# Seven products of a block in an order in which neighbours never share banks, and the convolution history turned in mid-block

## The chip, the cores and the metric

The kernel runs on one core of one Trainium2 chip. The metric is the time of one execution on the device in microseconds (us). The core has TensorE (matrix products, in the profile PE, and PEld for its weight loads), VectorE (DVE), ScalarE (ACT), GpSimd (POOL) and SyncE (SP), whose queue issues the transfers. Each engine works off its own list of instructions in order and waits for others through semaphores.

## What is computed

The reference is one inference step of a one-layer trunk with 1,024 prompt tokens and 8 x 4 sample tokens (`h` below is the normalised input, 1,056 tokens by 1,024 features). One projection of `h` feeds two branches; the second, a matrix memory with four heads, is the one that the change bears on:

```
pool_in, pool_z, qk_pre, v, o_pre, m_z, if_pre, gate_pre = jnp.split(h @ w_in, SPLIT_OFFSETS, axis=-1)
qk, conv_hist_new = causal_conv_silu(qk_pre, conv_hist, conv_w, conv_b)
q, k = jnp.split(qk, 2, axis=-1)

def causal_conv_silu(z, hist, w, b):
    S = z.shape[1]
    full = jnp.concatenate([hist.astype(z.dtype), z], axis=1)
    out = sum(full[:, j:j + S] * w[j] for j in range(CONV_W)) + b
    return jax.nn.silu(out), full[:, -(CONV_W - 1):]
```

`qk_pre` has 4,096 columns, `v`, `o_pre` and `m_z` 2,048 each, 512 for each head. The convolution has four taps, so that each sample sequence needs three rows of history (`state_conv`, 24 rows for 8 sequences), and the last three rows of each sequence are an output.

## The kernel before

The kernel runs in stages. The first, to about 950 us of the span, computes the ten thousand columns of `q`, `k`, `v`, `o_pre` and `m_z`; the stages behind it (gates, attention, the pooling branch, the output projections) are not touched.

**Blocks.** For each of the four heads there are seven blocks: `q` twice, `v`, `k` twice, `o`, `z` (line 1532 on). The blocks of `q` and `k` (ConvBlock, "feature blocks", 16 of them) put 256 output features on partitions and tokens on columns; those of `v`, `o` and `z` (TokBlock, "token blocks", 12) put tokens on partitions and 512 features on columns. A block is cut in two halves of tokens and two of features, and the four quarters are computed by Strassen and Winograd's scheme with seven products in place of eight. Every operand is kept as two parts, hi (`whi`, `hh`, `m2h`, ...) and lo (`wlo`, `hl`, `m2l`, ...), and a product is hi by hi, hi by lo and lo by hi: 24 matmuls of 264 columns in a feature block, and 48 matmuls of 256 columns in a token block.

**Products and banks.** The products are, by the letters of the new code, a (operand B11), 00 (B21), d (M1), b (M2), c (T3), 10 (N4) and 01 (B22). Each adds up in a pair of PSUM banks from `mm2()` (line 343; there are three pairs, `mm` in the trace). The "chain" pair takes a, then b, c and 10 on top of it; the pair `d` takes d and then 01; the pair `x` takes 00 alone. Before, the order is a, 00, d, b, c, 10, 01 (`run`, lines 76 to 103), so that b, c and 10, all of the chain, stand one behind the other. Behind a, b and c ScalarE copies the chain to SBUF (`save`, tile `s`: lines 158 to 161 in feature blocks, one instruction, and 215 to 219 in token blocks, two), and VectorE or ScalarE turns banks and saved sums into the four quarters (`bring`, tile `z`): quarter (0,0) from 00 and saved a, (1,1) from d's banks and saved c, (1,0) from the chain alone, (0,1) from d's banks after 01 and saved b.

**Weights.** `steps` (line 665) prepares the weights of a product three products ahead of it. `prep` adds and subtracts raw weight halves on VectorE; `split_w` makes `whi` on ScalarE (line 351) and `wlo` on VectorE (line 357), each in three rotating buffers. A feature block splits the weights of two products in one go: 00 with 10, d with b, 01 with c. The raw weights (`wraw`, seven buffers) come by DMA from SP's queue (line 653).

**Convolution.** When the weights of a feature block are asked for (`load`), `history` (line 269) also loads its 24 rows of history (tile `part`), turns them with two transposes on TensorE (line 277) and copies them to `hist`. `give` (line 285) puts the first three columns, the history and the samples in place on GpSimd and ScalarE, collects the rows of the new history in `new` on GpSimd (lines 297 and 300), and runs the taps on VectorE (line 305). At the end of the block `done` (line 312) turns `new` with two transposes (line 316) and stores it. Stores and loads share SP's queue.

**What sets the order.** The order in which the code is written is that of the products; a scheduler then places the instructions of each engine by simulated times, so that matmuls of the next block can stand between two products of this one.

Of the kernel before, what the change touches and what calls it, by code (L numbers as in the profile page):

```python
# [53 lines left out]
class Block:  # L54
# [7 lines left out]

    def __init__(self, tr, c0):
        self.tr, self.c0 = tr, c0
        self.w = [None] * 7
        self.saved = {}
        self.raw = [[], []]
        self.begin()
# [44 lines left out]
OPS = ("B11", "B21", "M1", "M2", "T3", "N4", "B22")  # L113


class FeatBlock(Block):


    def load(self, f):
        if f == 0:  # L120
            self.r = self.tr.raw_w(self.tr.I["w_in"], self.c0, 0)
            self.history()

    def history(self):
        pass

    def prep(self, i):
# [3 lines left out]
        if i == 0:  # L131
            self.w[0] = tr.split_w(r1[:, :, f1])
        elif i == 1:
            hi, lo = tr.split_w(r2)
            self.w[1], self.w[5] = [(hi[:, :, f], lo[:, :, f]) for f in (f1, f2)]
        elif i == 2:
# [4 lines left out]
            self.w[2], self.w[3] = [(hi[:, :, f], lo[:, :, f]) for f in (f1, f2)]  # L141
            tt(out=r1[:, :, f2], in0=r1[:, :, f1], in1=r1[:, :, f2], op=ALU.subtract)
            tt(out=r1[:, :, f1], in0=r2[:, :, f1], in1=x[:, :, f2], op=ALU.add)
        elif i == 4:
            hi, lo = tr.split_w(r1)
            self.w[6], self.w[4] = [(hi[:, :, f], lo[:, :, f]) for f in (f1, f2)]
# [11 lines left out]
    def save(self, name):  # L158
        tr = self.tr
        self.saved[name] = tr.t(tr.gp, [P, HH], "s", bufs=tr.nsb).rearrange("p (a n) -> p a n", a=2)  # L160
        tr.nc.scalar.activation(self.saved[name], self.chain[:, :, :CH], AF.Copy)
# [13 lines left out]
class TokBlock(Block):  # L175
# [15 lines left out]
    def prep(self, i):  # L191
        tr, r = self.tr, self.raw
        tt = tr.nc.vector.tensor_tensor
        if i == 2:
            self.x = tr.t(tr.wp, [P, 4, 256], "wraw", bufs=tr.nraw)
            tt(out=self.x, in0=r[0][1], in1=r[1][1], op=ALU.add)
        elif i == 3:
            tt(out=self.x, in0=r[0][0], in1=self.x, op=ALU.subtract)
        elif i == 4:
            tt(out=r[0][1], in0=r[0][0], in1=r[0][1], op=ALU.subtract)  # L200
        elif i == 6:
# [1435 lines left out]
```

## Time and profile before

| what | value |
|---|---|
| time, median of 3 runs | 2282.23 us (2280.12 to 2287.49) |
| the profiled execution, its time | 2283.02 us |
| its span in the profile | 2281.3 us |
| mean granted clock of TensorE | 0.987 of full speed |
| busy share TensorE, its weight loads | 95%, 90% |
| busy share VectorE, ScalarE, GpSimd | 55%, 41%, 6% |

The busy share is an average over all stages. A start time in a row of the timeline is in us from the start of the span; a name like `mm<-whi,t3h` says that the tile `mm` is written from the tiles `whi` and `t3h`; what stands in brackets is the idle time of the engine before the instruction and what ended it.

### The profile page before, as it was taken

The numbers are of one execution on the slowest core, as the hardware profiler recorded it, in microseconds if no ns is written. First come the engines' busy times: TensorE is split into PE (matmuls) and PEld (weight loads), VectorE is DVE, ScalarE is ACT, GpSimd is POOL, SyncE is SP. The second block draws the span as 40 slices with busy tenths as digits, with TensorE's granted clock in tenths as the row PEclk, the third lists the DMA queues.
The fourth block names the chain that finished last, engine by engine and source line by source line (L and its number), as shares of the span: only waits on it lengthen the run. The fifth ranks groups of instructions, "written<-read, shape, count | busy, mean of one in ns | idle before, by whom it ended". The sixth has DMA issues, their size and how long they took to land.

```text
span 2281.3 us, 39968 instructions
## 1 busy us (share of the span) xinstructions
PE 2162.9 (95%) x16311; PEld 2047.6 (90%) x16311; DVE 1259.2 (55%) x2168; ACT 927.3 (41%) x1796; POOL 136.1 (6%) x335
## 2 busy tenths in 40 slices
PE   4899999999999999999999999999998999999998
PEld 3899999999999999899999888878778999999998
DVE  7756465547554756435565765665582334443545
ACT  5536353635453546454333443322233331223443
POOL 1101010001000110000000000000000000000000
PEclk8999999999999999999999999999999999999999
DMA  3233323332323232384555563878674534324112
GB/s 127 80 109 102 112 77 108 101 107 82 108 92 98 93 97 74 95 271 153 185 179 163 172 192 121 300 247 287 249 241 173 171 96 130 104 70 138 52 47 82
DMA packets 238600, 312.70 MB, mean 137 GB/s; under 512 B 13994, under 2 KB 170066, under 8 KB 238416
## 3 DMA queue, kind: packets, MB, share of 16 engines
q1 hardware_dynamic: 238416, 310.15, 41.7%
q8 instruction: 128, 2.10, 0.4%
q14 instruction: 56, 0.46, 0.1%
HBM read 200.01 MB, written 110.45 MB: 136 GB/s over the span
## 4 chain that ended last, share of the span: by engine, by line
PE 83%; DMA 7%; ACT 3%; DVE 3%; SPq 1%; issue 1%; POOL 0%; DVEq 0%; POOLq 0%; ACTq 0%
PE mm L211 20%; PE mm L154 14%; PE mm L364 12%; PE mm L366 11%; PE mm L365 11%; PE num L1121 2%; PE misc L906 1%; PE num L364 1%; PE num L365 1%; PE num L366 1%; DMA o<-oD 1%; PE kv L364 1%; DMA ct<-state_mlstm_C 1%; PE kv L1125 1%; PE kv L365 1%
## 5 line engine op out<-in xcount | busy, mean ns | idle before, releaser
L357 DVE TENSOR_TENSOR wlo<-wraw,whi 128x1024 fp32r<-128x1024 f32 (+1 forms) x204 | 236.1, 1158 | 259.9 <-ACT whi L351 255.0
L351 ACT ACTIVATE whi<-wraw 128x1024 fp32r<-128x1024 f32 (+1 forms) x204 | 205.7, 1008 | 254.3 <-PE mm L365 91.4
L364 PE MATMUL mm<-hh,whi 128*128 128x352 f32 (+1 forms) x832 | 265.0, 319 | 13.4 <-ACT sz L1264 8.3
L366 PE MATMUL mm<-hh,wlo 128*128 128x352 f32 (+1 forms) x832 | 262.0, 315 | 0.0
L365 PE MATMUL mm<-hl,whi 128*128 128x352 f32 (+1 forms) x832 | 260.9, 314 | 0.0
L211 PE MATMUL mm<-whi,hh 128*128 128x256 f32 x768 | 216.5, 282 | 8.2 <-ACT whi L351 8.2
L211 PE MATMUL mm<-whi,hl 128*128 128x256 f32 x768 | 216.2, 281 | 0.0
L211 PE MATMUL mm<-wlo,hh 128*128 128x256 f32 x768 | 215.7, 281 | 0.0
L364 PEld LDWEIGHTS mm<-hh,whi 128*128 128x128 f32 x832 | 158.2, 190 | 27.4 <-ACT sz L1264 10.6
L365 PEld LDWEIGHTS mm<-hl,whi 128*128 128x128 f32 x832 | 158.7, 191 | 5.7 <-issue 4.4
L366 PEld LDWEIGHTS mm<-hh,wlo 128*128 128x128 f32 x832 | 158.2, 190 | 5.5 <-issue 4.2
L211 PEld LDWEIGHTS mm<-whi,hh 128*128 128x128 f32 x768 | 144.8, 189 | 13.2 <-ACT whi L351 9.9
L154 PE MATMUL mm<-hh,whi 128*128 128x264 f32 x512 | 148.8, 291 | 8.3 <-ACT whi L351 4.8
L305 DVE SCALAR_TENSOR_TENSOR z<-z,vcols,z 128x556 f32<-128x556 f32 x192 | 144.9, 792 | 17.6 <-ACT z L303 14.3
L154 PE MATMUL mm<-hl,whi 128*128 128x264 f32 x512 | 147.0, 287 | 1.5 <-DVE hl L359 1.2
L154 PE MATMUL mm<-hh,wlo 128*128 128x264 f32 x512 | 146.5, 286 | 0.0
L211 PEld LDWEIGHTS mm<-whi,hl 128*128 128x128 f32 x768 | 144.6, 188 | 0.0
L211 PEld LDWEIGHTS mm<-wlo,hh 128*128 128x128 f32 x768 | 144.4, 188 | 0.0
L1126 DVE SCALAR_TENSOR_TENSOR ct<-ct,dec,kv 128x512 f32<-128x512 f32 x128 | 93.3, 742 | 71.2 <-PE kv L1125 61.6
L366 PE MATMUL mm<-mvhB,wlo 128*128 128x352 f32 x384 | 122.9, 321 | 0.0
L365 PE MATMUL mm<-mvlB,whi 128*128 128x352 f32 x384 | 122.7, 321 | 0.0
L364 PE MATMUL mm<-mvhB,whi 128*128 128x352 f32 x384 | 121.6, 323 | 0.0
(439 smaller groups left out, 6087.8 us busy)
## 6 DMA issues: line engine op xcount, KB each, us to landing
wraw<-w_in SPq DMA_DIRECT2D x112, 512.0 KB
ct<-state_mlstm_C SPq DMA_DIRECT2D x32, 1024.0 KB
new_C_sample<-ct SPq DMA_DIRECT2D x32, 1024.0 KB
qkD<-z SPq DMA_DIRECT2D x64, 256.0 KB
qk<-qkD SPq DMA_DIRECT2D x16, 1024.0 KB
sgD<-sz SPq DMA_DIRECT2D x16, 528.0 KB
sg<-sgD SPq DMA_DIRECT2D x16, 528.0 KB
vD<-z SPq DMA_DIRECT2D x32, 256.0 KB
```

Of the source, the lines that this page charges most:

```text
L154: self.tr.nc.tensor.matmul(ps[:, j, :CH], lhsT=st[:, k], rhs=mv[k][:, c], start=start and k == 0 and n == 0, stop=stop and k == 3 and n == ...
L211: self.tr.nc.tensor.matmul(ps[:, t // 2, t % 2 * 256:t % 2 * 256 + 256], lhsT=st[k][:, c], rhs=mv[:, k], start=start and t % 2 == 0 and k ...
L305: nc.vector.scalar_tensor_tensor(out=acc, in0=z[:, o:o + tot], scalar=wc(o), in1=acc, op0=ALU.mult, op1=ALU.add)
L351: self.nc.scalar.activation(out, in_, AF.Copy)
L357: self.nc.vector.tensor_tensor(out=out, in0=in_, in1=hi.bitcast(F32), op=ALU.subtract)
L364: mm(ps, lhsT=sh, rhs=mh, start=start, stop=False)
L365: mm(ps, lhsT=sh, rhs=ml, start=False, stop=False)
L366: mm(ps, lhsT=sl, rhs=mh, start=False, stop=stop)
L906: nc.tensor.matmul(out, lhsT=qk[:, 4 + d, i * L:(i + 1) * L], rhs=qk[:, d, i * L:], start=d == 0, stop=d == 3)
L1121: nc.tensor.matmul(num[32 * d:32 * d + 32, 0, :], lhsT=qm[:, b * P + d * NS:b * P + (d + 1) * NS], rhs=ct[:, d, :], start=b == 0, stop=b = ...
L1125: nc.tensor.matmul(kv, lhsT=km[:, d * P:(d + 1) * P], rhs=vst, start=True, stop=True)
L1126: nc.vector.scalar_tensor_tensor(out=ct[:, d, :], in0=ct[:, d, :], scalar=self.dec[:, h * DB + b, 1:2], in1=kv, op0=ALU.mult, op1=ALU.add)
```

## The change

The seven products come in the order a, d, b, 00, c, 01, 10 (in the first block of all a, 00, d, b, c, 01, 10), so that two neighbours never use the same pair of banks. With it, the saved sums are a, d and b in place of a, b and c: quarter (1,1) is now taken from the chain's banks after c, with the saved d. Preparation goes by names of products; in feature blocks 00 and 10 are split by themselves (two splits of 128x512 for one of 128x1024), the sums for c move from the preparation of d to that of c. The history's load stays where it was, and its transposes and its copy move to the place just before product 00. Buffers of `s` go from 5 to 6, of `zc` from 6 to 3.

```
+    order = ("a", "d", "b", "00", "c", "01", "10")
...
     def run(self, i):
         tr = self.tr
-        if i == 0:
+        if i == "a":
             self.chain = tr.mm2()
-            self.product(self.chain, 0, True, False)
-            self.save("a")
-        elif i == 1:
+            self.product(self.chain, i, True, False)
+            self.save(i, self.chain)
+        elif i == "d":
+            self.d = tr.mm2()
+            self.product(self.d, i, True, False)
+            self.save(i, self.d)
+        elif i == "b":
+            self.product(self.chain, i, False, False)
+            self.save(i, self.chain)
+        elif i == "00":
             x = tr.mm2()
-            self.product(x, 1, True, True)
+            self.product(x, i, True, True)
             self.take(0, 0, x, "a")
-        elif i == 2:
-            self.d = tr.mm2()
-            self.product(self.d, 2, True, False)
-        elif i == 3:
-            self.product(self.chain, 3, False, False)
-            self.save("b")
-        elif i == 4:
-            self.product(self.chain, 4, False, False)
-            self.save("c")
-            late = self.bring(1, 1, self.d, "c")
-            self.late = late
-        elif i == 5:
-            self.product(self.chain, 5, False, True)
+        elif i == "c":
+            self.product(self.chain, i, False, False)
+            self.late = self.bring(1, 1, self.chain, "d")
+        elif i == "01":
+            self.product(self.d, i, False, True)
+            self.take(0, 1, self.d, "b")
+        else:
+            self.product(self.chain, i, False, True)
             self.take(1, 0, self.chain, None)
             self.give(1, 1, self.late)
-        else:
-            self.product(self.d, 6, False, True)
-            self.take(0, 1, self.d, "b")
             self.done()
...
     def load(self, f):
         if f == 0:
             self.r = self.tr.raw_w(self.tr.I["w_in"], self.c0, 0)
-            self.history()
+            self.history_load()
...
-        elif i == 1:
-            hi, lo = tr.split_w(r2)
-            self.w[1], self.w[5] = [(hi[:, :, f], lo[:, :, f]) for f in (f1, f2)]
-        elif i == 2:
+        elif i == "00":
+            self.w["00"] = tr.split_w(r2[:, :, f1])
+        elif i == "10":
+            self.w["10"] = tr.split_w(r2[:, :, f2])
+        elif i == "d":
...
+    def run(self, i):
+        if i == "00":
+            self.history()
+        super().run(i)
...
-            self.last[f] = tr.t(g, [P, 3], "zc", bufs=6)
+            self.last[f] = tr.t(g, [P, 3], "zc", bufs=3)
...
+        blocks[0].order = ("a", "00", "d", "b", "c", "01", "10")
+        todo = [(b, n, i) for b in blocks for n, i in enumerate(b.order)]
...
-        self.nraw, self.nsb, self.nz = 7, 5, 7
+        self.nraw, self.nsb, self.nz = 7, 6, 7
```

Two places show how instructions move. The first is TensorE in the token block `v` of head 1. Before, mm_473_3493 is the chain's pair of banks; m2, t3 and n4 are the operands of b, c and 10, and misc is the bank of the history's transposes:

```order
L211 MATMUL mm_473_3493<-whi_3547,m2l_414 128x256
L277 MATMUL misc_3809<-ident_112,part_3807 128x24 [waits DMAHW7_49,PE_49]
L277 MATMUL misc_3809<-ident_112,part_3807 128x24
L277 MATMUL misc_4099<-ident_112,part_4097 128x24 [waits DMAHW0_49,DVE_49]
L277 MATMUL misc_4099<-ident_112,part_4097 128x24
L211 MATMUL mm_473_3493<-whi_3631,t3h_411 128x256 [waits Activation_49]
...
L211 MATMUL mm_473_3493<-whi_3631,t3l_412 128x256
L211 MATMUL mm_473_3493<-whi_3684,n4h_140_455 128x256 [waits Activation_49]
L211 MATMUL mm_473_3493<-wlo_3685,n4h_140_455 128x256 [waits DVE_49]
```

After, in the same block, mm_485_3518 is the chain, mm_502_3714 the pair of 00 and mm_490_3575 that of d:

```order
L215 MATMUL mm_485_3518<-whi_3514,m2l_412 128x256
L215 MATMUL mm_502_3714<-whi_3571,hh_135 128x256 [waits PE_49,Activation_49]
L215 MATMUL mm_502_3714<-wlo_3572,hh_135 128x256 [waits DVE_49]
...
L215 MATMUL mm_485_3518<-whi_3653,t3h_409 128x256 [waits Activation_49]
...
L215 MATMUL mm_485_3518<-whi_3653,t3l_410 128x256
L215 MATMUL mm_490_3575<-whi_3710,hh_135 128x256 [waits Activation_49]
...
L215 MATMUL mm_485_3518<-whi_3769,n4h_140_453 128x256 [waits DVE_49,Activation_49]
```

Between b and c of the chain now stands product 00, between c and 10 product 01, and the history's transposes are gone from this block. The first matmul of 10 waits for VectorE, which reads the chain's banks behind c, as well as for its weights.

The second place is TensorE in a `k` block of head 1. Before, mm_514_3940 is the chain, and mm_547_4219 the banks of a of the next block:

```order
L154 MATMUL mm_514_3940<-m2h_413,whi_3934 128x264 [waits Activation_49]
...
L154 MATMUL mm_547_4219<-hh_135,whi_4103 128x264 [waits DVE_49,Activation_49]
L154 MATMUL mm_547_4219<-hl_136,whi_4103 128x264
L154 MATMUL mm_514_3940<-t3h_411,whi_4008 128x264 [waits Activation_49]
...
L154 MATMUL mm_547_4219<-hh_135,wlo_4104 128x264 [waits DVE_49]
...
L154 MATMUL mm_514_3940<-n4h_140_455,whi_3873 128x264 [waits Activation_49]
```

After, mm_521_3952 is the chain, mm_533_4048 the banks of 00, mm_525_3983 those of d, mm_556_4235 those of the next block's a, and misc_4228 the bank into which `new` is turned:

```order
L157 MATMUL mm_521_3952<-m2h_411,whi_3892 128x264 [waits Activation_49]
...
L157 MATMUL mm_533_4048<-hl_136,whi_3979 128x264
...
L157 MATMUL mm_525_3983<-hh_135,whi_4012 128x264 [waits Activation_49]
...
L157 MATMUL mm_521_3952<-t3h_409,whi_4012 128x264 [waits Activation_49]
...
L157 MATMUL mm_556_4235<-hh_135,whi_4125 128x264 [waits DVE_49,Activation_49]
...
L157 MATMUL mm_521_3952<-n4h_140_453,whi_4089 128x264 [waits DVE_49]
...
L328 MATMUL misc_4228<-ident_112,new_4042 27x128 [waits Pool_49]
```

Before, the one or two first matmuls of the next block stand between b and c; after, 17 matmuls of 00 and 12 of 01 stand there, and 12 of 01 and 18 of the next a between c and 10. The first of the two transposes of `new` stands behind 10, and the second about 30 matmuls later.

## Rows read from the trace of the kernel before

**Rows 1.** The page: busy us, share and instructions by engine; granted clock in 40 slices.

```profile
PE 2162.9 (95%) x16311; PEld 2047.6 (90%) x16311; DVE 1259.2 (55%) x2168; ACT 927.3 (41%) x1796; POOL 136.1 (6%) x335
...
PEclk8999999999999999999999999999999999999999
```

**Rows 2.** Stretch, length; busy us (x) of PE, PEld, DVE, ACT, POOL; clock; DMA share; GB/s.

```profile
100.00:935.00 835.00, 802.61 (x6805) 779.26 (x6804) 476.04 (x573) 407.04 (x718) 63.92 (x175) 1.00 0.30 94
```

**Rows 3.** Waits of TensorE, 100 to 935 us: total us, times, longest us.

```profile
PE mm L211 <- ACT s L219: 16.6, 18, 1.2
...
PE mm L211 <- ACT whi L351: 7.2, 7, 1.0
...
PE mm L154 <- ACT whi L351: 4.2, 7, 0.6
...
PE misc L277 <- DMA part<-state_conv: 3.5, 5, 1.4
```

**Rows 4.** Timeline, c and 10 of a token block: start, us, engine, line, instruction, idle before.

```profile
348.77 0.39 PE L211 MATMUL mm<-whi,t3h 128*128 128x256 f32 x1 [0.21 <-ACT s L219]
...
354.43 0.28 PE L211 MATMUL mm<-whi,t3l 128*128 128x256 f32 x1
355.88 0.39 PE L211 MATMUL mm<-whi,n4h 128*128 128x256 f32 x1 [1.18 <-ACT s L219]
...
354.74 1.09 ACT L219 ACTIVATE s<-mm 128x512 f32<-128x512 f32 x2 [4.88 <-PE mm L211]
```

**Rows 5.** Timeline, end of b in the two feature blocks of a pair.

```profile
378.82 0.28 PE L154 MATMUL mm<-m2h,wlo 128*128 128x264 f32 x1
379.70 0.39 PE L154 MATMUL mm<-hh,whi 128*128 128x264 f32 x1 [0.60 <-ACT whi L351]
...
379.02 0.63 ACT L351 ACTIVATE whi<-wraw 128x512 fp32r<-128x512 f32 x1 [0.44 <-PE mm L154]
...
400.58 0.29 PE L154 MATMUL mm<-m2h,wlo 128*128 128x264 f32 x1
401.89 0.38 PE L211 MATMUL mm<-whi,hh 128*128 128x256 f32 x1 [1.02 <-ACT whi L351]
402.39 0.39 PE L154 MATMUL mm<-t3h,whi 128*128 128x264 f32 x1
```

**Rows 6.** Groups by form, 100 to 900 us, splits: busy us, mean ns; idle before, releasers.

```profile
L351 ACT ACTIVATE whi<-wraw 128x1024 fp32r<-128x1024 f32 x121 | 128.1, 1059 | 132.6 <-PE mm L211 59.7 <-PE mm L154 55.1 <-issue 13.0
...
L351 ACT ACTIVATE whi<-wraw 128x512 fp32r<-128x512 f32 x14 | 8.8, 630 | 3.2 <-PE mm L154 3.2
...
L357 DVE TENSOR_TENSOR wlo<-wraw,whi 128x1024 fp32r<-128x1024 f32 x121 | 147.8, 1221 | 175.8 <-ACT whi L351 175.1
...
L357 DVE TENSOR_TENSOR wlo<-wraw,whi 128x512 fp32r<-128x512 f32 x14 | 9.6, 686 | 13.3 <-ACT whi L351 13.3
```

**Rows 7.** What `new` waits for: groups, 100 to 900 us; line L300 (shortest/median/longest ns); its transposes.

```profile
L168 ACT ACTIVATE z<-mm 128x528 f32<-128x528 f32 x15 | 8.9, 590 | 0.0
...
L300 POOL COPY new<-z 128x12 f32<-128x12 f32 x58 | 29.8, 513 | 0.0
L294 POOL COPY zc<-z 128x3 f32<-128x3 f32 x29 | 17.3, 598 | 338.2 <-DVE z L170 254.9 <-ACT z L168 83.3
...
L300 POOL COPY new<-z x64: 188/196/1917, 41.2 to 857.6; 128x12 f32<-128x12 f32 x64
...
198.37 0.38 PE L316 MATMUL misc<-ident,new 128*27 128x128 f32 x2
```

**Rows 8.** Waits of SP's queue and VectorE, 100 to 935 us: total us, times, longest us.

```profile
SPq L653 <- DVE wlo L357: 209.3, 46, 12.2
...
DVE wraw L138 <- DMA wraw<-w_in: 7.2, 5, 2.3
```

**Rows 9.** Timeline of TensorE at the start: the history of the first block, and transposes behind it.

```profile
24.48 0.38 PE L277 MATMUL misc<-ident,part 24*128 24x24 f32 x2 [3.29 <-DMA part<-state_conv]
...
28.40 0.69 PE L542 MATMUL mm<-ident,t3h 128*128 128x128 f32 x2 [2.16 <-ACT n4h L564]
```

More of the change, by code (lines that the diff above doesn't have):

```diff
@@ L121, in load, with history_load @@
             self.r = self.tr.raw_w(self.tr.I["w_in"], self.c0, 0)
-            self.history()
-    def history(self):
+            self.history_load()
+    def history_load(self):
         pass
@@ L140, in prep @@
             hi, lo = tr.split_w(x)
-            self.w[2], self.w[3] = [(hi[:, :, f], lo[:, :, f]) for f in (f1, f2)]
+            self.w["d"], self.w["b"] = [(hi[:, :, f], lo[:, :, f]) for f in (f1, f2)]
+            self.x = x
+        elif i == "c":
             tt(out=r1[:, :, f2], in0=r1[:, :, f1], in1=r1[:, :, f2], op=ALU.subtract)
-            tt(out=r1[:, :, f1], in0=r2[:, :, f1], in1=x[:, :, f2], op=ALU.add)
-        elif i == 4:
+            tt(out=r1[:, :, f1], in0=r2[:, :, f1], in1=self.x[:, :, f2], op=ALU.add)
             hi, lo = tr.split_w(r1)
-            self.w[6], self.w[4] = [(hi[:, :, f], lo[:, :, f]) for f in (f1, f2)]
+            self.w["01"], self.w["c"] = [(hi[:, :, f], lo[:, :, f]) for f in (f1, f2)]
     def product(self, ps, i, start, stop):
@@ L156, in product, with save @@
                                              skip_group_check=True)
-    def save(self, name):
+    def save(self, name, ps):
         tr = self.tr
         self.saved[name] = tr.t(tr.gp, [P, HH], "s", bufs=tr.nsb).rearrange("p (a n) -> p a n", a=2)
-        tr.nc.scalar.activation(self.saved[name], self.chain[:, :, :CH], AF.Copy)
+        tr.nc.scalar.activation(self.saved[name], ps[:, :, :CH], AF.Copy)
     def out(self, dst, ps, other, func=AF.Copy):
@@ L193, in prep @@
         tt = tr.nc.vector.tensor_tensor
[L194 removed]
+        if i == "d":
             self.x = tr.t(tr.wp, [P, 4, 256], "wraw", bufs=tr.nraw)
             tt(out=self.x, in0=r[0][1], in1=r[1][1], op=ALU.add)
[L197 removed]
+        elif i == "b":
             tt(out=self.x, in0=r[0][0], in1=self.x, op=ALU.subtract)
[L199 removed]
+        elif i == "c":
             tt(out=r[0][1], in0=r[0][0], in1=r[0][1], op=ALU.subtract)
[L201 removed]
+        elif i == "01":
             tt(out=self.x, in0=r[1][0], in1=self.x, op=ALU.add)
[L203 removed]
+        self.w[i] = tr.split_w(r[0][0] if i == "a" else r[1][0] if i == "00" else r[0][1] if i == "c" else
+                               r[1][1] if i == "10" else self.x)
     def product(self, ps, i, start, stop):
@@ L213, in product, with save @@
                                              stop=stop and k == 3 and n == 2, skip_group_check=True)
-    def save(self, name):
+    def save(self, name, ps):
         tr = self.tr
@@ L218, in save @@
         for j, x in enumerate(self.saved[name]):
-            tr.nc.scalar.activation(x, self.chain[:, j], AF.Copy)
+            tr.nc.scalar.activation(x, ps[:, j], AF.Copy)
     def sample(self):
@@ L267, in begin, with history_load @@
         self.last = {}
+    def history_load(self):
+        tr, nc, g = self.tr, self.tr.nc, self.tr.gp
+        self.h1 = tr.t(g, [P, 512], "part", bufs=2)[:24, :256]
+        nc.sync.dma_start(self.h1, tr.I["state_conv"][:, :, self.cols].rearrange("b j f -> (b j) f"))
+    def run(self, i):
+        if i == "00":
+            self.history()
+        super().run(i)
     def history(self):
@@ L272, in history @@
         self.hist = tr.t(g, [P, 2, 24], "hist", bufs=2)
-        h1 = tr.t(g, [P, 512], "part", bufs=2)[:24, :256]
-        nc.sync.dma_start(h1, tr.I["state_conv"][:, :, self.cols].rearrange("b j f -> (b j) f"))
         ps = tr.miscps()
         for f in range(2):
-            nc.tensor.transpose(ps[:, f * 24:(f + 1) * 24], h1[:, f * P:(f + 1) * P], tr.ident[:24, :24])
+            nc.tensor.transpose(ps[:, f * 24:(f + 1) * 24], self.h1[:, f * P:(f + 1) * P], tr.ident[:24, :24])
         nc.scalar.activation(self.hist, ps[:, :48].rearrange("p (f r) -> p f r", f=2), AF.Copy)
@@ L665, in steps @@
     def steps(self, blocks):
-        todo = [(b, i) for b in blocks for i in range(7)]
+        blocks[0].order = ("a", "00", "d", "b", "c", "01", "10")
+        todo = [(b, n, i) for b in blocks for n, i in enumerate(b.order)]
         made = 0
-        for n, (b, i) in enumerate(todo):
+        for n, (b, _, i) in enumerate(todo):
             while made < min(len(todo), n + (2 if n < 2 else 3)):
-                x, j = todo[made]
-                if j == 0:
-                    x.load(0)
-                if j == 1:
-                    x.load(1)
-                if j == 4:
+                x, k, j = todo[made]
+                if k < 2:
+                    x.load(k)
+                if k == 4:
                     x.sample()
```

9 lines of the change are left out of this document (4 added, 5 removed).

## The prediction

> **What bounds the kernel now.** I read the page's busy shares first. TensorE's matmuls fill 95% of the span, VectorE 55%, ScalarE 41%, and the granted clock is at its upper level, 2.4 GHz, in nearly every slice [rows 1]. So a microsecond taken from TensorE's idle time in the projection stage is a microsecond of the result, as long as nothing else becomes late. Then I cut the span by stage. The change touches the stage of the 28 projection blocks only, from about 30 to 950 us. In its even part, 100 to 935 us, matmuls are busy 802.61 of 835 us at a granted clock of 1.00 [rows 2]. The list of what TensorE waited for in that part has four lines and no more [rows 3]: the saves of a bank (s, L219) 16.6 us in 18 waits, the high halves of the weights (whi, L351) 7.2 and 4.2 us in 7 waits each, and the convolution history arriving by DMA (L277) 3.5 us in 5. Those are 31.5 us, and each line is something that the change moves.
>
> The idle figure of a row starts at a modelled end of the matmul before, so I measured by starts. Within a token block, 47 steps lie between 348.77 and 354.43, 0.120 us each; the next matmul starts at 355.88, 1.45 later: 1.33 us lost where the row says 1.18 [rows 4]. ScalarE shows why. The product "c" ends, the save of its two banks runs from 354.74 for 1.09 us, and "10" can write these banks only behind the first half of it. In the feature blocks the same place, "b" followed by "c", loses 0.76 us in the first block of a pair (378.82 to 379.70) and 1.19 + 0.38 in the second (400.58 to 401.89 to 402.39) [rows 5]. The scheduler put one or two matmuls of the next block there as a filler, and their own weights are late: their whi buffer comes free only when "b" ends, and ScalarE takes 0.63 or 1.06 us for the split.
>
> **The change part by part.** *Order of products, token blocks (12).* No two neighbours share banks any more: d stands between a and b, 00 between b and c, 01 between c and 10. Each of these products is 48 matmuls of 0.120 us, 5.8 us; the saves take 1.09 us, so about 4.5 us of cover is left. Removed: the 16.6 us of the saves, plus 0.15 us for each of the 9 waits with no transpose before them (the difference of 1.33 and 1.18), 18.0 us.
>
> *Order of products, feature blocks (16).* Between b and c there now stand 29 matmuls (17 of 00, 12 of 01), between c and 10 about 30 (12 of 01, 18 of the next a): 3.5 and 3.6 us of cover for a save of one 0.6 us instruction behind a split of 0.63. The next block's a comes only after 01 has begun, long after its buffer is free. Removed: 0.76 + 1.19 + 0.38 = 2.33 us per pair, 8 pairs (the first before 100 us), 18.6 us.
>
> *The history turned in mid-block.* Its load is issued where it was, three products ahead of the block; its two transposes move behind a and d of their own block, where only the copy to hist and the give of 00 want them. On SP nothing is passed that was not before it: the load still waits behind the weight loads. The 3.5 us of waits for its DMA go. In the head the same wait is 3.29 us [rows 9], but the transposes behind it wait for ScalarE later anyway, 2.16 us at 28.40 [rows 9]. Its worth there lies between 0 and 3.3; I take 1.5, about the middle.
>
> *What is added.* In a feature block the weights of 00 and 10 are split in two pieces instead of one: 16 times two ScalarE instructions of 630 ns for one of 1059, +0.20 us each, 3.2 us; and two VectorE ones of 686 ns for one of 1221, +0.15 us, 2.4 us [rows 6]. ScalarE is busy 407 and VectorE 476 of 835 us [rows 2], so both are hidden; if that cover were gone they would cost 5.6 us. The save of d replaces the save of c, so the number of saves stays. The two transposes of new stood together, and now stand apart, 32 interruptions of the product stream for 16. A pair is 0.38 us of TensorE [rows 7], 0.2 us each; the transposes' own time is there before and after, so one more break costs between 0 and, I estimate, one transpose's 0.2 us. I take 0.1, 1.6 us in all. The buffers s grow from 5 to 6, which the three live saves of a token block need (two tiles each), and zc shrinks from 6 to 3, a tile that is dead when its block is done.
>
> *What could be new.* The transposes of new come 42 and 30 matmuls behind the products that feed them (5.0 and 3.6 us), where before the pair had over 50 (6 us) and never waited. What must fit: ScalarE's split 0.63 and copy 0.59, then GpSimd's copies zc and new, 0.60 and 0.51 us in the mean, the longest new 1.92 [rows 6, 7]. That is 2.3 us in the mean and 3.7 with the longest copy, against 3.6 us; the trace of before shows no such wait, so it costs 0 to about 1 us per block, 0 to 16 us in all. The mean fits, so I lean to the lower end and take 4.
>
> Sum: -18.0 - 18.6 - 3.5 - 1.5 + 1.6 + 4 = -36.0 us. Against the profiled execution's 2283.02 us that gives 2247.0; it lies 0.8 us above the median of the runs, 2282.23, so the forecast for the median is 2246.
>
> **The rivals.** *A: GpSimd's copies hold up the transposes.* Each feature block then waits at the second transpose of new, and the saving shrinks by the 12 us between the 4 that I took and the 16 of the upper bound: 2258, up to 2264 if the first transpose waits too. For it: copies of the same 128x12 vary from 188 to 1917 ns [rows 7], so something delays them. The Trainium skill's page "SBUF — State Buffer", section "Who interferes with whom", has a rule by which this goes on: a VectorE instruction with two SBUF inputs and a GpSimd one that reads SBUF exclude each other, the later one blocking for a whole instruction; the convolution's VectorE instructions have two SBUF inputs, and the spread of the copies agrees with it. By that rule the upper end, 2258, is where the time would lie. Against it: the median copy is 0.20 us, and a wait of 1 us per block needs the worst case each time.
>
> *B: VectorE's read of the chain comes late; slower than before.* The (1,1) sum used to be read from d's banks, with no hurry. Now VectorE reads it from the chain's own banks, and 10 must wait for that. It writes a z buffer, which must be free, so its last store must have landed, and stores share SP's queue with weight loads that wait for their buffers up to 12.2 us, 209.3 us in 46 waits [rows 8]. If a store sat behind such a load, VectorE's queue would stand and with it 10: 12.2 minus the cover of 3.6 is 8.6 us. At 2.3 us per feature block (36/16) the whole gain is gone; at 3 us it gives 2294. Against it: VectorE's waits in this part name a DMA only for raw weights, 7.2 us in 5 [rows 8], and never for a z buffer.
>
> *C: the waits move, so that the order does not do what it says.* Taking a save out of the way brings forward the next thing that ScalarE or VectorE owes, the split of the weights in three rotating whi buffers. If each of the 28 blocks met a wait of 1.0 us there, as the feature blocks do now, the gain would be 36 - 28 = 8 us: 2274. If it met 1.3, nothing would be left, 2282. Against it: whi is wanted two products after its buffer comes free, 5.8 us or more, and split and residue take 1.06 + 1.22 = 2.3 us [rows 6].
>
> **How the numbers follow.** Forecast (waits gone, new ones under 8 us): 2238 to 2255, 0.70. Rival A: 2255 to 2266, 0.14. Rival C: 2266 to 2287, 0.10, half of it below 2275. Rival B: 0.04. A gain beyond 40 us (the head giving its 3.3 us, no new wait, and the 0.1 us that each restart costs saved too): 0.02. The range reaches from 2237, every removed term with no new cost, to 2264, A's end, and leaves out about 2 in 10. What a measurement here can tell from no change is about 0.3%, 6.8 us. Faster by more: forecast, A, and most of C, 0.91. Within: the end of C, 0.05. Slower: B, 0.04.
>
> **What would show it.** Right: in the part from about 100 us on, TensorE's waits have no line for s and none for the history's DMA; whi stays under 2 us; matmuls busy about 98% of that stage, which is some 36 us shorter, and everything behind it starts that much earlier. Wrong by A: waits of the transposes of new for GpSimd, or for ScalarE's copy before it. By B: the first matmul of 10 waiting for VectorE's z, and VectorE for a store. By C: whi or wlo with more than 10 us. The stages behind 960 us should keep their lengths within 2 us; if they do not, the step that takes them as unchanged is wrong.

## The result and the profile after

The changed kernel takes 2243.5 us (2240.4 to 2244.9), against 2281.2 us before on the same chip: a ratio of 0.983, with a 95% interval of 0.981 to 0.985. The forecast was 2246. The page of its profiled execution (2243.27 us, span 2241.5) answers to [rows 1]: busy us and share by engine, then the granted clock in 40 slices.

```profile
PE 2154.4 (96%) x16311; PEld 2045.7 (91%) x16311; DVE 1267.6 (57%) x2184; ACT 903.5 (40%) x1796; POOL 120.2 (5%) x335
...
PEclk8999999999999999999999999999989999999999
```

As many matmuls as before, and less time around them. The stretch that answers to [rows 2], with as many matmuls in it, 6,805, is 793 us long in place of 835 (columns as there), and TensorE is busy in all of it:

```profile
100.00:893.00 793.00, 792.70 (x6805) 776.99 (x6803) 477.74 (x583) 381.59 (x712) 45.24 (x172) 1.00 0.32 99
```

The waits of TensorE from 100 to 935 us answer to [rows 3]. None of the four lines of before is left; what stands there is the gate rows and the seam to the next stage, at about 909 us (total us, times, longest us):

```profile
PE mm L376 <- ACT whi L363: 4.8, 1, 4.8
PE mm L721 <- DVE z L725: 1.7, 2, 0.9
PE mm L378 <- DVE wlo L369: 0.3, 1, 0.3
```

The timeline of a token block shows the places of [rows 4]: 00, c, 01 and 10 follow one another without a break, 0.12 us from start to start (columns start, us, engine, line, instruction). The save of b (L223) runs beside 00, and VectorE reads c's banks (L246) beside 01:

```profile
333.24 0.28 PE L215 MATMUL mm<-whi,hl 128*128 128x256 f32 x1
333.36 0.28 PE L215 MATMUL mm<-whi,t3h 128*128 128x256 f32 x1
...
338.94 0.28 PE L215 MATMUL mm<-whi,t3l 128*128 128x256 f32 x1
339.06 0.28 PE L215 MATMUL mm<-whi,hh 128*128 128x256 f32 x1
...
344.56 0.28 PE L215 MATMUL mm<-whi,hl 128*128 128x256 f32 x1
344.67 0.28 PE L215 MATMUL mm<-whi,n4h 128*128 128x256 f32 x1
...
327.87 1.09 ACT L223 ACTIVATE s<-mm 128x512 f32<-128x512 f32 x2 [2.40 <-PE mm L215]
...
339.26 1.29 DVE L246 TENSOR_TENSOR z<-mm,s 128x512 f32<-128x512 f32 x2 [3.28 <-PE mm L215]
```

In a feature block, the place of [rows 5], 00 follows the last matmul of b after 0.13 us from start to start, where the next matmul came after 0.88 and 1.31 us before (378.82 to 379.70, 400.58 to 401.89):

```profile
360.23 0.29 PE L157 MATMUL mm<-m2h,wlo 128*128 128x264 f32 x1
360.36 0.29 PE L157 MATMUL mm<-hl,whi 128*128 128x264 f32 x1
```

The last matmul of the blocks starts 42.85 us earlier than before; from there to the end the changed kernel is 3.05 us longer, with the same 9,007 matmuls. The first two rows are the last product matmul, before and after; the next two the stretch from it to the end of the span, before and after (columns as in [rows 2]).

```profile
947.10 0.28 PE L211 MATMUL mm<-whi,hl 128*128 128x256 f32 x1
...
904.25 0.28 PE L215 MATMUL mm<-whi,n4l 128*128 128x256 f32 x1
...
947.10:2281.30 1334.20, 1283.44 (x9007) 1199.60 (x9005) 706.97 (x1462) 462.99 (x966) 57.55 (x123) 0.99 0.50 166
...
904.25:2241.50 1337.25, 1285.43 (x9007) 1200.24 (x9005) 708.16 (x1456) 462.87 (x966) 58.54 (x127) 0.98 0.50 166
```

So 2283.02 - 42.85 + 3.05 is 2243.2; the changed kernel's profiled execution took 2243.27. The total is not a clean reading of a term of a few microseconds. The start of the last product matmul is a better one: each kernel was traced once, and in six that hardly differ in the blocks (the changed one and five of those below) it lies between 903.11 and 904.61, a spread of 1.5 us. The experiments are read by both.

### The profile page after: what moved, and what is told of

Read it like the earlier page. It is cut to its first block, busy times and chain, and to the rows that moved or that the text cites. A ratio compares the mean times of both kernels' runs of the same rounds, so it can differ in the third digit from the quotient of the medians.

```text
span 2241.5 us, 40008 instructions
## 1 busy us (share of the span) xinstructions
PE 2154.4 (96%) x16311; PEld 2045.7 (91%) x16311; DVE 1267.6 (57%) x2184; ACT 903.5 (40%) x1796; POOL 120.2 (5%) x335
## 4 chain that ended last, share of the span: by engine, by line
PE 87%; DMA 6%; DVE 3%; ACT 2%; issue 1%; SPq 1%; POOL 0%; DVEq 0%; POOLq 0%; ACTq 0%
PE mm L215 21%; PE mm L157 15%; PE mm L376 12%; PE mm L378 12%; PE mm L377 12%; PE num L1132 2%; PE misc L917 1%; PE num L376 1%; PE num L377 1%; PE kv L1136 1%; PE num L378 1%; DMA o<-oD 1%; PE kv L376 1%; DMA ct<-state_mlstm_C 1%; PE kv L377 1%; PE kv L378 1%
```

## The experiments

### Each part alone: the order, the history

The first kernel has the new order and everything else of the change, but turns the history where the kernel before does, right behind its load:

```
     def load(self, f):
         if f == 0:
             self.r = self.tr.raw_w(self.tr.I["w_in"], self.c0, 0)
             self.history_load()
+            self.history()
...
-    def run(self, i):
-        if i == "00":
-            self.history()
-        super().run(i)
```

> The changed kernel with the history's transposes left where the kernel before has them (asked for with the load, three products ahead of the block); the new order of products and everything else as changed. Theory (each removed wait was paid by itself): the five waits for the history's transfer, 3.5 us, come back and the head loses up to 1.5 us, so 2243.5 + 3.5 to 5 = 2247 to 2248.5. Rival (the order of products is all that counts, the transfer was waited for in the shadow of the saves): 2243 to 2245, and TensorE shows no wait for the history above 0.5 us.

Measured: 2243.8 us, last product at 903.82 us, 0.43 us before that of the changed kernel, and no wait for the history from 100 us on; in the head one of 2.08 us is left, 2.54 in the changed kernel. The rival holds: moving the history adds nothing to the new order.

The second is the kernel before with the history moved to just before product 00:

```
-            self.history()
+            self.history_load()
...
+    def run(self, i):
+        if i == 1:
+            self.history()
+        super().run(i)
```

> The kernel before with one part of the change alone: the history's transposes moved to just before product 00. Theory: the 3.5 us of waits for the transfer go, the waits for the saves stay, 2281.2 - 3.5 = 2277.7 (2276 to 2279). Rival: the transposes stood between b and c, where TensorE waits for the save of b anyway, so that without them the wait for the save grows by as much: 2280 to 2282, with the waits for s (18.0 us) longer than before. The two parts together should add up: what this run gains and what the order alone gains should make 37.7 us.

Measured: 2286.6 us, a ratio of 1.0018 (1.0006 to 1.0031) to the kernel before; the last product starts at 949.84, 2.74 us later than before. Its waits from 100 to 935 us:

```profile
PE mm L211 <- ACT s L219: 20.5, 20, 1.2
PE mm L211 <- ACT whi L359: 7.2, 7, 1.0
PE mm L154 <- ACT whi L359: 4.2, 7, 0.6
PE misc L285 <- DMA part<-state_conv: 0.2, 1, 0.2
```

Beside [rows 3]: the wait for the transfer is gone, 3.5 to 0.2 us, and the waits for the saves have grown by 3.9. The transposes had filled the gap in which TensorE waited for the save of b. In the three places that lost them (258.69, 479.00 and 699.91 us before) the gap stays at 1.33 us, now without anything in it: most of the wait for the transfer stood in the shadow of another wait. Only in two places had the transfer made the gap longer, to 1.60 and 1.95 us, so that 0.9 of the 3.5 us was to be had. And the transposes now cost time of their own: in seven feature blocks they stand with those of `new`, where nothing is waited for, and the step that lost 0.13 us loses 0.54, 2.8 us in all. The two make 2.0 of the 2.2 us by which the stage is longer from 100 us on (table below).

### Token blocks and feature blocks

In each of these two, one class of blocks gets back the order a, 00, d, b, c, 10, 01 with saves of a, b and c; the other keeps the new one:

```
 class TokBlock(Block):
...
+    order = ("a", "00", "d", "b", "c", "10", "01")
...
+        elif i == "c":
+            self.product(self.chain, i, False, False)
+            self.save(i, self.chain)
+            self.late = self.bring(1, 1, self.d, "c")
```

> The changed kernel with the 12 token blocks in the order of before (a, 00, d, b, c, 10, 01, saving a, b and c); the feature blocks keep the new order. Theory (the terms add up, token blocks carry 18.0 us of the stage's 42.9): the waits for s at the first matmul of 10 come back, 12 times 1.2 to 1.33 us plus some at c, and the stage of blocks ends 16 to 20 us later, so 2260 to 2264. Rival (the feature blocks carry nearly all of it, as the swap of saves alone already emptied most token waits): under 8 us, 2244 to 2252.

> The changed kernel with the 16 feature blocks in the order of before (a, 00, d, b, c, 10, 01, saving a, b and c), the token blocks in the new one: the counterpart of the run with old token blocks. Theory (the terms add up): the late whi behind b come back, 2.33 us per pair, 18.6 us, so that the stage of blocks ends 17 to 23 us later: 2260 to 2267; with the 21.9 us of the other run they make the stage's 42.9. Rival (the new order of token blocks alone also frees ScalarE for the splits of the feature blocks next to them): under 10 us, 2244 to 2254.

Measured: with old token blocks 2269.8 us (2258.5 to 2277.2), last product at 926.13; with old feature blocks 2268.1 us, last product at 927.81. So the new order is worth 21.0 us in feature blocks alone (947.10 - 926.13) and 19.3 us in token blocks alone (947.10 - 927.81); together 40.3 us, and the whole change gave 42.85. The terms add up to within 2.6 us. Both stages end a little later than the theory said, 21.9 us behind the changed kernel where it had 16 to 20, and 23.6 where it had 17 to 23, and both totals lie above its range. Their waits in the blocks, first with old token blocks, then with old feature blocks, are those of [rows 3], split in two:

```profile
PE mm L244 <- ACT s L252: 20.3, 20, 1.2
PE misc L318 <- DMA part<-state_conv: 0.5, 2, 0.3
```

```profile
PE mm L244 <- ACT whi L392: 7.2, 7, 1.0
PE mm L186 <- ACT whi L392: 4.2, 7, 0.6
```

### Is it the neighbours, or that nothing else was ready?

The first test makes one pair of neighbours share banks again, in the changed kernel (whose first block of all has b next to c anyway):

```
-    order = ("a", "d", "b", "00", "c", "01", "10")
+    order = ("a", "d", "b", "c", "00", "01", "10")
```

> The changed kernel with the order a, d, b, c, 00, 01, 10: one pair of neighbours, b and c, uses the same banks again, in all 28 blocks but the first. Theory (neighbours on the same banks cost a save each): 12 token blocks at 1.33 us and 15 feature blocks at 0.76 to 1.57 us come back, 27 to 40 us, so 2271 to 2283. Rival (what counts is that another product is ready to be slipped in between): the order of instructions shows 30 matmuls of 00 between b and c in token blocks and 22 or more in feature blocks, so nothing comes back but the late weights of 00 in front of b, where only two matmuls stand: 2243 to 2250.

Measured: 2259.2 us. In this run the sample rows of the token blocks were computed with weights that c's preparation had already overwritten; the next one takes that product one step earlier.

> The changed kernel with the order a, d, b, c, 00, 01, 10 once more, and the sample rows' product taken one step earlier, so that it uses the weights before c's preparation overwrites them (in the run before they were overwritten). Theory (neighbours on the same banks cost a save each): 27 to 40 us come back, 2271 to 2283. Rival (what counts is a ready product, after the run before): the stage of blocks is 6 to 12 us longer than that of the changed kernel, 2250 to 2260, with no line of waits for s above 3 us and TensorE waiting for GpSimd's new, since the first transpose of new then stands only 6 matmuls behind 10.

Measured: 2258.7 us, last product at 914.86, 10.6 us later than in the changed kernel, where theory had 27 to 40 more. Its waits from 100 to 893 us hold one single wait for a save, in the last token block; elsewhere the scheduler put other matmuls between b and c, 26 to 30 of 00 in a token block, 29 of other products in a feature block. The other line is rival A's: the first transpose of `new` now stands 6 matmuls behind 10, and waits for GpSimd in 7 blocks. One of these in the timeline follows. By the method of the table below, the steps with transposes lose 4.5 us more than in the changed kernel, the save in the last token block 1.3, the sample product (32 small matmuls for the sample rows of a token block), which the scheduler tore apart in four blocks, 2.5, and small steps and the end of the last block 2.7.

```profile
PE misc L328 <- POOL new L312: 3.4, 7, 0.5
PE mm L215 <- ACT s L223: 1.2, 1, 1.2
...
293.41 0.29 PE L328 MATMUL misc<-ident,new 128*27 128x128 f32 x1 [0.48 <-POOL new L312]
```

The second test keeps the old order and changes only which sums are saved, in the kernel before: d in place of c. Then 01, on d's banks, may start as soon as d is saved.

```
         elif i == 2:
             self.d = tr.mm2()
             self.product(self.d, 2, True, False)
+            self.save("d", self.d)
...
         elif i == 4:
             self.product(self.chain, 4, False, False)
-            self.save("c")
-            late = self.bring(1, 1, self.d, "c")
+            late = self.bring(1, 1, self.chain, "d")
```

> The kernel before with its order a, 00, d, b, c, 10, 01, and only the saves changed: d is saved in place of c, and quarter (1,1) is read from the chain's banks with the saved d (buffers of s 6 and zc 3, as in the changed kernel). Product 01 can then start as soon as d is saved. Theory (the order of the products is what removes the waits): b, c and 10 still follow one another in the code, so the waits stay: 2276 to 2284. Rival (what counts is that another product is ready): the order of instructions now has 32 matmuls of 01 between c and 10 in token blocks, and 24 of 01 behind b in feature blocks, so the 18 us of the token blocks go at least in part, and some of the 18.6 us of the feature blocks: 2250 to 2268, and the waits of TensorE for s fall below 6 us.

Measured: 2263.9 us, last product at 922.89, 24.2 us earlier than before, with the products in the old order in the code. Its waits from 100 to 909 us:

```profile
PE mm L211 <- ACT whi L351: 7.2, 7, 1.0
PE mm L211 <- ACT s L219: 5.4, 8, 1.2
PE misc L277 <- DMA part<-state_conv: 1.8, 4, 0.6
PE mm L211 <- DVE wlo L357: 0.4, 1, 0.4
```

The waits for saves fall from 16.6 to 5.4 us and the 4.2 us of L154 vanish; the 7.2 us of the second block of a pair stay, where the filler is the next block's a with late weights. More than half of the change's gain, 24.2 of 42.85 us, is that another product is ready, not that the code names it next.

All of this can be put in one table. It is worked out from TensorE's timeline: the time from one start of a product matmul to the next, less 0.120 us (the median step) for each matmul, summed from 100 us to the last product, and sorted by what stands in the step. The second line holds the steps of over 0.3 us; smaller ones are in the last but one.

| us lost from 100 us on | before | history alone | d saved | token old | feature old | changed |
|---|---|---|---|---|---|---|
| at c or 10, token blocks, nothing else in the step | 12.0 | 16.0 | 1.3 | 16.0 | 0 | 0 |
| from b to c, feature blocks | 16.3 | 16.3 | 11.0 | 0 | 16.3 | 0 |
| steps with transposes of history or `new` | 16.2 | 14.1 | 12.6 | 12.5 | 7.1 | 5.4 |
| steps with the sample product or gate rows | 31.8 | 31.8 | 31.2 | 31.8 | 33.5 | 33.5 |
| all other steps (some 6,300) | 3.0 | 3.3 | 0.6 | 1.1 | 1.7 | 0.2 |
| sum (before rounding) | 79.3 | 81.5 | 56.7 | 61.3 | 58.7 | 39.1 |

### Details of the change: separate splits, the sixth s, the z buffers

```
         elif i == "00":
-            self.w["00"] = tr.split_w(r2[:, :, f1])
-        elif i == "10":
-            self.w["10"] = tr.split_w(r2[:, :, f2])
+            hi, lo = tr.split_w(r2)
+            self.w["00"], self.w["10"] = [(hi[:, :, f], lo[:, :, f]) for f in (f1, f2)]
```

> The changed kernel with one detail undone: in feature blocks the weights of 00 and 10 are split in one piece again, so that this whi buffer is held from 00 to 10, the last product of the block. Theory (the separate splits cost nothing and are what keeps whi off the path): the buffer comes free only behind 10, and d of the next block, which is wanted about 6 matmuls (0.7 us) later, waits for a split of 1.06 us: 0.8 to 1.4 us in some 8 to 16 blocks, 6 to 20 us, so 2250 to 2264, with waits of TensorE for whi. Rival (the third buffer is enough): 2242 to 2245, and ScalarE and VectorE some 5 us less busy.

Measured: 2241.5 us, last product at 904.43 (changed: 904.25), and no wait for whi in the blocks. The rival holds: the split in two pieces is neither needed nor paid for. ScalarE is busy 377.27 us from 100 to 893, 4.3 less than with separate splits, and nothing comes of it.

```
-        self.nraw, self.nsb, self.nz = 7, 6, 7
+        self.nraw, self.nsb, self.nz = 7, 5, 7
```

> The changed kernel with 5 buffers s in place of 6. A token block has three live saves of two tiles, so that the second tile of b waits until VectorE has read the first tile of a, which it does behind 00. Theory (six are needed): c waits for that save, 1.0 to 1.3 us in 12 token blocks, 12 to 16 us, so 2255 to 2260. Rival (another product is slipped in: the order of instructions has 35 matmuls of 01 ahead of c in a token block): under 4 us, 2243 to 2248.

Measured: 2260.3 us, last product at 914.26, 10.0 us later; in the traces the time behind the blocks is 7.3 us longer too, so that the total comes near the theory's by chance alone. The theory's mechanism is not there: c does not wait for the save, and from 100 to 893 us TensorE has no wait at all. The rival's time is missed too. The 10 us are elsewhere. In the steps with the sample product 28.9 us are lost for 23.5: with one buffer fewer the scheduler tore the sample product of four of the twelve token blocks in three. In the timeline of TensorE, the sample product whole in one block, and torn in the next:

```profile
615.77 1.93 PE L700 MATMUL misc<-wraw,hs 128*32 128x256 f32 x32
...
640.44 1.91 PE L700 MATMUL misc<-wraw,hs 128*32 128x256 f32 x26
642.60 0.62 PE L700 MATMUL misc<-wraw,hs 128*32 128x256 f32 x2
660.19 0.63 PE L700 MATMUL misc<-wraw,hs 128*32 128x256 f32 x4
```

32 matmuls take 1.93 us in one go; 26, 2 and 4 of them take 3.16 us.

In the steps with the gate rows, at the end of the stage, 14.2 us are lost for 10.1, and here, behind 893 us, TensorE does wait. The gate rows read `hh` and `hl` of the plain input, which are made from four sums in tiles `s` (line 651). In the changed kernel VectorE works on two of the sums at a time and has the last `hl` at 890.66 us; with five buffers it makes one after the other, the last at 901.75. TensorE waits for the last `hh` and `hl`, 2.0 and 0.4 us, and then the granted clock falls to its lower level, 1.2 GHz, in a part of the stretch behind, where the changed kernel keeps 1.00 to the end of the blocks. The first row is the wait for `hh`, the second that stretch (columns as in [rows 2]):

```profile
PE mm L721 <- ACT hh L363: 2.0, 1, 2.0
...
901.00:910.00 9.00, 7.66 (x37) 7.15 (x38) 4.29 (x10) 1.63 (x5) 0.00 (x0) 0.62 0.00 1
```

```
-        self.nraw, self.nsb, self.nz = 7, 6, 7
+        self.nraw, self.nsb, self.nz = 7, 6, 5
```

> The changed kernel with 5 buffers z in place of 7, TensorE's order unchanged. It asks how near the rival stands by which VectorE reads the chain too late because it waits for a z buffer whose store sits in SP's queue. Theory (that wait is far off): 2242 to 2247, no wait of 10 for VectorE. Rival: VectorE waits for stores, 10 starts late, 2 to 3 us in each of 16 feature blocks, so 2275 to 2290.

Measured: 2245.3 us, last product at 903.72, no wait for VectorE's z but that of the gate rows (L721). Rival B is far off: two buffers fewer don't bring it up. The time behind the blocks is 5.5 us longer than in the changed kernel, with the same instructions there; of this, below.

### A faster version

The largest wait left is at the seam: 4.78 us for the next stage's first weights, whose load stands in SP's queue behind stores of the gate rows and of the last block.

```
-            nc.sync.dma_start(self.g8D[:, t0:t0 + n], g8[:, :n])
+            nc.gpsimd.dma_start(self.g8D[:, t0:t0 + n], g8[:, :n])
...
-            self.tr.nc.sync.dma_start(
+            (self.tr.nc.gpsimd if self.kind == "z" and self.h == 3 else self.tr.nc.sync).dma_start(
```

> A try for a faster version: the changed kernel with the stores of the gate rows (g8D) and of the last block (zD) on GpSimd's queue in place of SP's. In the changed kernel the last big wait of the stage is 4.94 us at its end, where the next stage's first weights are loaded at 903.05 us, behind those stores on SP, and split at 908.20. Theory (the load is late because of what stands ahead of it on SP): it is issued some 15 us earlier, and the wait shrinks to the split, 1.1 to 2.5 us: 2239 to 2242. Rival (the load waits for its buffer, not for the queue): no change, 2243 to 2245, or later if GpSimd's queue is slow.

Measured: 2246.5 us, no gain. The load is issued 16 us earlier, at 886.81 in place of 903.05, and the first matmul waits 2.12 us, as the theory had it. But the fifth matmul, the first that reads a low half, then waits 5.09 us for VectorE. Its timeline at the seam, with TensorE's two waits first and VectorE's rows below:

```profile
907.00 0.43 PE L376 MATMUL mm<-hh,whi 128*128 128x352 f32 x1 [2.12 <-ACT whi L363]
...
913.38 0.66 PE L378 MATMUL mm<-hh,wlo 128*128 128x352 f32 x1 [5.09 <-DVE wlo L369]
...
907.64 3.77 DVE L505 TENSOR_SCALAR cmask<-tri 128x128 f32<-128x128 f32 x1 [2.10 <-POOL tri L502]
907.78 4.29 DVE L512 TENSOR_TENSOR smask<-tri,bcol 32x32 f32<-32x32 f32 x4
912.10 1.23 DVE L369 TENSOR_TENSOR wlo<-wraw,whi 128x1024 fp32r<-128x1024 f32 x1
```

VectorE makes masks ahead of the low halves; they wait for a tile that GpSimd makes, and GpSimd now issues the stores first. Most of the wait is the masks themselves: `cmask` takes 3.77 us here (3.76 in the changed kernel), 0.25 in the kernel before and 0.23 in the last version. GpSimd fills tiles with constants beside it in both long cases, but in the kernel before as well, so why it is long is not shown. So the last version also makes the masks in the middle of the blocks; to find room for them it takes 6 buffers z, and it splits 00 and 10 in one piece:

```
+            if n == 100:
+                self.masks()
...
-        self.mk, _m = self.pool("mask", "right")
-        self.masks()
-        _m.close()
...
-        self.nraw, self.nsb, self.nz = 7, 6, 7
+        self.nraw, self.nsb, self.nz = 7, 6, 6
```

> A try for a faster version: stores of the gate rows and of the last block on GpSimd's queue (so that the next stage's first weights are loaded early), the masks made in the middle of the stage of blocks in place of its end (so that VectorE is free for the low halves of those weights), 00 and 10 split in one piece, and 6 buffers z to make room. Theory: the waits at the seam of the stages, 4.78 and 0.32 us in the changed kernel and 2.12 and 5.09 with the queue alone, shrink to 2 to 3.5 us together: 1.5 to 3 us faster than the changed kernel, 2239 to 2242. Rival: the seam shrinks and the time is given back later, where stretches of TensorE's idle time and of a lower granted clock differ by up to 5 us between these kernels: 2243 to 2247.

Measured: 2236.2 us (2235.0 to 2238.7), a ratio of 0.981 (0.979 to 0.982) to the kernel before. Its waits at the seam, 893 to 912 us, and its `cmask`:

```profile
PE mm L375 <- ACT whi L362: 2.1, 1, 2.1
PE mm L721 <- DVE z L725: 0.9, 1, 0.9
PE mm L377 <- DVE wlo L368: 0.4, 1, 0.4
...
456.21 0.23 DVE L505 TENSOR_SCALAR cmask<-part 128x128 f32<-128x128 f32 x1
```

The waits for the next stage's weights are 2.5 us together, 5.1 in the changed kernel: 2.6 gained there, and 1.1 in the blocks (last product at 903.11), which is within the spread of 1.5. The median is 7.3 us below that of the changed kernel, but on another chip, where the kernel before took 2279.7 us; by the ratios the difference is 0.0021, 4.8 us, and the two intervals overlap. What goes beyond the seam is in the stages behind. It beats the kernel before; that it beats the changed one by more than the seam's 2.6 us is not shown.

## Why the prediction was right, step by step

**Bound and stage.** Right: what TensorE lost in the blocks came off the time.

**Saves, 18.0 us.** Right in the place, but in size only together with the history's 3.5 us. From 100 us on nineteen places lost a save's 1.33 us. Nine have nothing else in the step, 12.0 us (first line of the table). Ten have history transposes in it, of which the prediction counted the idle remainder alone; two of these were longer by the transfer, and the ten lost 14.2 us. Against this stands what the prediction gave no price: in the gaps the history's transposes cost nothing, in their new place a pair costs 0.32 us, 4.5 us for 14 pairs. 12.0 + 14.2 - 4.5 is 21.7 us, where the prediction had 18.0 + 3.5 = 21.5; that the two sums agree is luck in part. Token blocks alone gave 19.3. One reading is off, and nothing hangs on it: 10 starts behind the whole save of c (355.83 and 355.88 in [rows 4]), not behind its first half.

**Late whi behind b, 18.6 us.** Right: 16.3 from 100 us on and 2.33 in the first pair; feature blocks alone gave 21.0, with small waits of the table's last line but one, among them 0.15 us between filler and c in the first block of each pair.

**The history, 3.5 and 1.5 us.** Wrong as a step. The wait for the transfer did go, but by the new order, which goes without it wherever the transposes stand; the move by itself gained nothing on top of the order and lost 2.7 us without it. I took a row of waits as time to be saved, and asked of the saves, but not of this row, what would be late next: the save of b. Nor did I ask what the transposes cost where nothing is waited for. In the head the move gained nothing that shows either: 2.54 us of wait at 25.28 are left of the 3.29 of [rows 9], since in the first block 00 comes second, and 2.08 with the transposes in their old place.

```profile
25.28 0.38 PE L289 MATMUL misc<-ident,part 24*128 24x24 f32 x2 [2.54 <-DMA part<-state_conv]
```

**Extra splits hidden.** Right, by their removal.

**Interruptions +1.6 and GpSimd's copies +4.** Both too dear. Before, 15 steps with a pair of `new` lost 0.13 us each, 2.0 us; now 23 steps with a single one lose 0.02 each, and seven that share a step with a history pair 0.05 each, 0.9 us in all. Apart they are cheaper, by 1.1 us. (The rest of the 5.4 us in the table's third line is the history's pairs.) No transpose of `new` waits: from the end of the last copy into `new` to the transpose, the least is 1.77 us. In the timeline of one block, GpSimd, VectorE and TensorE:

```profile
312.04 0.74 POOL L306 COPY zc<-z 128x3 f32<-128x3 f32 x1 [5.17 <-ACT z L171]
312.73 0.19 POOL L312 COPY new<-z 128x12 f32<-128x12 f32 x1
312.86 1.19 POOL L308 COPY z<-zc 128x3 f32<-128x3 f32 x1
...
311.52 1.23 DVE L369 TENSOR_TENSOR wlo<-wraw,whi 128x1024 fp32r<-128x1024 f32 x1
312.78 1.23 DVE L205 TENSOR_TENSOR wraw<-wraw,wraw 128x1024 f32<-128x1024 f32 x1
...
314.69 0.27 PE L328 MATMUL misc<-ident,new 128*27 128x128 f32 x1
```

The copy zc ends when VectorE's instruction does (312.78, 312.75), the last copy likewise (314.05, 314.01); the copy to `new` slips in between in 0.19 us. All 43 of these copies that are longer than 0.4 us in the changed kernel run beside a VectorE instruction with two SBUF inputs. The Trainium skill's page "SBUF — State Buffer", section "Who interferes with whom", says that a VectorE instruction with two SBUF inputs contends with a GpSimd instruction that reads SBUF, over a shared pair of ports that is an exclusive lock. The trace agrees with that mechanism, with these ends. Rival A's price was wrong all the same: the copies to `new` have a mean of 191 ns now, 513 before [rows 7]. That the new order puts them at other moments is the likely reason, not one that a run tested. That such waits can come was seen in the run with b then c, where 6 matmuls of cover are not enough.

```profile
L312 POOL COPY new<-z 128x12 f32<-128x12 f32 x57 | 10.9, 191 | 0.0
```

**What I left out.** The table's last line but one: 3.0 us in some 6,300 steps, each a small loss of under 0.2 us, fell to 0.2; the sample product and the gate rows lost 1.7 more. Sum of the stage from the table, 40.2 us, and 2.6 us before 100 us: 42.85, where I had 36.0. Of the 6.85 us between, 5.6 are the two costs that did not come.

**The stages behind, unchanged within 2 us.** Wrong as a bound: 3.05 us longer. In the traces of the twelve kernels above that leave these stages as they are (all but the last two), they take 1333.2 to 1344.6 us, with the same 9,007 matmuls. So the change's 3.05 is no effect that I can show. It is also why a forecast 6.85 us off in its stage came within 3.8 us of the profiled time (2247.0 and 2243.27) and 2.5 us of the median: that much is luck.

**Rivals B and C** did not happen: no wait for a z of the blocks (the two of L721 are the gate rows'), and whi only at the seam.

## What to carry to other kernels

A row of waits is worth its time only if nothing else stands behind it in the same gap: ask of each row what is late next, and add up parts that share a gap only once. Work that stands in a gap is free there, and costs its own time where it is moved to. List the waits to the very end of a stage: those of the run with five buffers s stood in its last 20 us. When an engine waits to re-use a buffer, look first for another piece of work that could stand there and why it isn't ready; saving a different operand (24 of 43 us here) may free it without any new order, and a fixed order then makes it sure. Read a change of one stage at the end of that stage, not at the end of the kernel.

## What the runs showed that was not expected

The stages behind the blocks vary by some 11 us between traces with the same instructions there. This need not be the kernels: each was traced once, and the kernel before alone took 2276.41 to 2288.02 us in the 13 runs beside the first experiments, with a mean granted clock of 0.990 and 0.983 at the two ends. A part of it is the granted clock: the same stretch of 28 us held 175 matmuls at 1.00 in the kernel before, all of it at the upper level, 2.4 GHz, and 164 at 0.94 with the history moved, some of it at the lower one, 1.2 GHz, after a wait of 2.69 us where the kernel before has 1.58. The first row is of the kernel before, the second of that with the history moved (columns as in [rows 2]):

```profile
1792.00:1820.00 28.00, 28.00 (x175) 28.00 (x176) 8.54 (x17) 11.79 (x27) 0.00 (x0) 1.00 0.39 118
...
1795.00:1823.00 28.00, 27.68 (x164) 27.68 (x165) 8.93 (x17) 11.71 (x27) 0.00 (x0) 0.94 0.35 106
```

And a product of small matmuls is cheap only in one piece: torn in three, the 32 of the sample product went from 1.93 to 3.16 us. In four blocks that made up over half of the 10 us that one buffer s fewer cost, without a wait in the list.
